# Down projection with seven products instead of eight, its operand sums made in gate and up, a new pool layout and row sums of squares

## The chip, the cores and the metric

The kernel runs on one core of a Trainium2 chip. The metric is the time of one execution on the device in microseconds. The kernel is a whole layer stack of two blocks for 512 tokens of width 2048; the change touches only its last part: the second output projection, the gate and up projections of the second block's feed-forward network, and the down projection with the final norm.

## The reference, cut to what matters

All arrays are float32. After the second block's mixer the reference computes, with `x` the residual stream of 512 x 2048 and `h` the mixer's output:

```python
x = x + h @ w_out_2                              # second output projection
y = rmsnorm(x, norm2_g_2)
u = silu(y @ ffn_w_gate_2) * (y @ ffn_w_up_2)    # 2048 -> 5632, gate and up
x = x + u @ ffn_w_down_2                         # 5632 -> 2048, down
out = rmsnorm(x, final_norm_g_2)
```

`rmsnorm` divides a row by the root of its mean square (plus 1e-6) and multiplies by a weight for each column.

## The kernel before, in words

Every float32 product is made of three matmuls in the fp32r type. Each operand is split into a high part (a cast by ScalarE, `split` at L136) and a low part (what is left, a subtraction by VectorE, `tt` at L122), and high x high, high x low and low x high are summed in PSUM. Weights come as blocks of 256 x 512 (a tile of 128 x 1024, 512 KB) on SP's DMA queue and are split into `wh` and `wl`, here called a weight half. Instructions are put in order by a scheduler that follows priorities (`high_priority`), and each engine then works through its own list in order. Two tiles of different pools may lie at the same bytes when their lifetimes don't overlap; the later one waits for the earlier.

`finish` holds the part that matters here.

- **Second output projection.** Four blocks of 512 features (b = 0, 2, 1, 3). For each, TensorE makes four tiles of 128 features x 512 tokens; VectorE adds the residual (`xr`), scales to `z`, and TensorE turns the tile to token rows, which ScalarE copies to `xs` and a DMA writes to `x3d`. The sum of squares of each token is collected in feature layout: ScalarE squares each tile, VectorE adds it to `s3` (`squares`), and at the end eight small matmuls with ones and `token_rsq` give `r3`. After each pair of blocks `fast_operands` builds the operands of the seven products for gate and up.
- **Gate and up.** Eleven chunks of 512 hidden features. Each product of a 2 x 2 block matrix is made by seven block products instead of eight (`fast_group`), with the sums of raw weights made by VectorE in place (`chained`) and the results combined from PSUM. `X` holds the operands, `fr` the raw weights, ten buffers; the weight halves rotate over three buffers (`wps`: two of `wp2`, one of `fw`). The activations come out in token rows, are turned by TensorE and written as 4 x 11 feature tiles to `ud` in DRAM.
- **Down.** `hidden(c)` reads a chunk of `ud` and splits it. `down(c, hs)` goes over four column blocks of 512; for each, `block` loads two weight halves and makes 4 row tiles x 4 token tiles x 3 matmuls, and VectorE adds the four PSUM tiles to `facc`, which starts as the residual read back from `x3d`. The weight halves rotate over the two buffers of `wp2`, the raw weights over three. The last chunk has its weights split ahead, and goes token tile by token tile with the final norm behind it.

Of the kernel before, what the change touches and what calls it, by code (L numbers as in the profile page):

```python
# [8 lines left out]
F32 = mybir.dt.float32  # L9
F32R = mybir.dt.float32r  # L10
# [7 lines left out]
D = 2048  # L18
# [75 lines left out]
class Kernel:  # L94
# [1508 lines left out]
    def fast_operands(self, pool, za, zb, tiles):  # L1603
        ta, tb = slice(0, 256), slice(256, 512)
        x5 = self.t(pool, [128, 4, 256], F32, "fx5")
        x6 = self.t(pool, [128, 4, 256], F32, "fx6")
        x7 = self.t(pool, [128, 4, 256], F32, "fx7")
# [4 lines left out]
        for i, x in ((1, za[:, :, ta]), (7, x7), (5, x5), (6, x6), (4, None), (3, zb[:, :, tb]), (2, zb[:, :, ta])):  # L1612
            if i == 4:
                x = x7
                self.tt(x, zb[:, :, ta], x6, ALU.add)
# [7 lines left out]
    def halves(self, raw, pools):  # L1623
# [4 lines left out]
        return h, l  # L1628

    def fast_group(self, srcs, X, rp, cp, wps, parts):
# [22 lines left out]
        def part(i, u, opens):  # L1655
            with tc.high_priority(self.ahead):
                h, l = self.halves(weight[i](u), wps)
            at = [(2 * u + kk, kk, t) for kk in range(2) for t in range(2)]

            for j, kk, t in at:  # L1660
                xh, xl = (x[:, j % 4, t * 128:t * 128 + 128] for x in X[j // 4][i])
                self.mm(ps[i][:, t, :], xh, h[:, kk, :], opens and j == 0, False, not opens)
                self.mm(ps[i][:, t, :], xl, h[:, kk, :], False, False, not opens)
            for j, kk, t in at:
                xh = X[j // 4][i][0][:, j % 4, t * 128:t * 128 + 128]
                self.mm(ps[i][:, t, :], xh, l[:, kk, :], False, j == 7, not opens)
# [43 lines left out]
    def finish(self):  # L1710
        tc, nc, a = self.tc, self.nc, self.a
        NC = 11
        ud = self.t(self.dr, [4 * NC, 128, NX], F32, "ud")
        x3d = self.t(self.dr, [4, 128, D], F32, "x3d")
        wg, wu, wd = a["ffn_w_gate_2"][0], a["ffn_w_up_2"][0], a["ffn_w_down_2"][0]
        with self.pool("ff0", 1) as f0:
# [3 lines left out]
            with self.pool("opx", 2) as opx:  # L1720
                X = []
                made = [0]

# [4 lines left out]
                with self.pool("w21", 1) as p1, self.pool("w22", 2) as p2, self.pool("w23", 3) as p3:  # L1728
                    s3 = self.t(p1, [128, NX], F32, "s3")
                    R1 = self.token_row(p1, self.r1, "R1")  # L1730
                    za = None
                    for n, b in enumerate((0, 2, 1, 3)):
# [6 lines left out]
                        for j in range(4):  # L1739
# [6 lines left out]
                            s = self.t(p2, [128, NX], F32, "sq")  # L1746
                            self.squares(s3, x3, n == 0 and j == 0, s)
# [135 lines left out]
```

## Time and profile before

| | us |
|---|---|
| median of 3 runs | 3528.63 (3527.05 to 3533.05) |
| the profiled execution | 3531.79 |
| its span, first to last instruction | 3530.0 |
| second output projection, gate and up | TensorE changes over at about 2137 to 2155 of the span |
| gate and up, down | TensorE changes over at about 3025 to 3045 of the span |

The span of the profiled execution was recorded instruction by instruction. TensorE's granted clock was 0.985 of full speed in the mean. Busy times of TensorE overlap from one matmul to the next, so what counts there is the distance from start to start.

### The profile page before, as it was taken

The numbers are of one execution on the slowest core, as the hardware profiler recorded it, in microseconds if no ns is written. First come the engines' busy times: TensorE is split into PE (matmuls) and PEld (weight loads), VectorE is DVE, ScalarE is ACT, GpSimd is POOL, SyncE is SP. The second block draws the span as 40 slices with busy tenths as digits, with TensorE's granted clock in tenths as the row PEclk, the third lists the DMA queues.
The fourth block names the chain that finished last, engine by engine and source line by source line (L and its number), as shares of the span: only waits on it lengthen the run. The fifth ranks groups of instructions, "written<-read, shape, count | busy, mean of one in ns | idle before, by whom it ended". The sixth has DMA issues, their size and how long they took to land.

```text
span 3530.0 us, 48454 instructions
## 1 busy us (share of the span) xinstructions
PE 3438.7 (97%) x18738; PEld 2740.7 (78%) x18738; DVE 2213.8 (63%) x3495; ACT 1367.9 (39%) x2223; POOL 55.1 (2%) x50
## 2 busy tenths in 40 slices
PE   6999999999999999999999998999999999999998
PEld 3488888777778787788777786888888888788887
DVE  4367875466555455764566557778887788555545
ACT  3234444465433323433233334444444444322122
POOL 0000000000000000000000000000000000000000
PEclk8999999999999999999999999999999999999999
DMA  8833433222343443434434543444334335533333
GB/s 283 276 90 89 113 115 109 70 80 63 88 149 124 138 131 97 116 108 132 132 105 144 163 137 108 131 128 123 114 108 125 120 114 160 185 119 119 102 96 108
DMA packets 352602, 442.21 MB, mean 125 GB/s; under 512 B 45871, under 2 KB 200179, under 8 KB 351731
## 3 DMA queue, kind: packets, MB, share of 16 engines
q1 hardware_dynamic: 349456, 437.82, 40.8%
q8 instruction: 147, 2.41, 0.3%
q10 hardware_dynamic: 2915, 1.29, 0.1%
q14 instruction: 84, 0.69, 0.1%
HBM read 383.45 MB, written 55.57 MB: 124 GB/s over the span
## 4 chain that ended last, share of the span: by engine, by line
PE 90%; DMA 5%; DVE 3%; issue 1%; ACT 1%; SPq 0%; POOL 0%; DVEq 0%; POOLq 0%; ACTq 0%
PE acc L112 41%; PE psm L112 23%; PE pp L112 23%; DMA wm<-in_w_mod_dram 2%; PE psm L116 2%; DVE wl L122 1%; PE pt L116 1%; DMA xr<-in_x_dram 0%; DMA raw<-in_ffn_w_down_dram 0%; DVE ga L132 0%; DMA ym<-ysd 0%; DMA fr<-in_ffn_w_gate_dram 0%; DVE op L122 0%; DMA xr<-in_ctx_dram 0%; DMA fr<-in_ffn_w_up_dram 0%
## 5 line engine op out<-in xcount | busy, mean ns | idle before, releaser
L112 PE MATMUL acc<-op,wh 128*128 128x512 f32 (+2 forms) x4160 | 1245.0, 389 | 12.2 <-ACT op L136 4.1
L112 PEld LDWEIGHTS acc<-op,wh 128*128 128x128 f32 (+1 forms) x4160 | 765.1, 190 | 198.8 <-issue 32.2
L122 DVE TENSOR_TENSOR wl<-raw,wh 128x512 fp32r<-128x512 f32 (+4 forms) x464 | 420.8, 907 | 631.6 <-ACT wh L136 597.9
L112 PE MATMUL acc<-op,wl 128*128 128x512 f32 (+2 forms) x2080 | 768.3, 389 | 4.9 <-DVE wl L122 4.7
L136 ACT CAST wh<-raw 128x512 fp32r<-128x512 f32 (+4 forms) x464 | 369.1, 796 | 991.4 <-PE acc L112 597.5
L112 PE MATMUL pp<-wh,op 128*128 128x512 f32 x2112 | 529.7, 393 | 10.1 <-ACT wh L136 10.1
L136 ACT CAST wh<-fr 128x1024 fp32r<-128x1024 f32 x308 | 322.9, 1052 | 400.8 <-PE pp L112 352.8
L112 PEld LDWEIGHTS pp<-wh,op 128*128 128x128 f32 x2112 | 397.5, 188 | 98.8 <-ACT wh L136 10.2
L112 PEld LDWEIGHTS acc<-op,wl 128*128 128x128 f32 (+1 forms) x2080 | 389.7, 189 | 98.9 <-issue 18.5
L122 DVE TENSOR_TENSOR wl<-fr,wh 128x1024 fp32r<-128x1024 f32 x308 | 371.0, 1219 | 103.8 <-ACT wh L136 67.0
L112 PE MATMUL psm<-wh,op 128*128 128x512 f32 x1280 | 396.6, 391 | 7.3 <-DVE facc L122 7.3
L112 PEld LDWEIGHTS psm<-wh,op 128*128 128x128 f32 x1280 | 241.6, 189 | 58.2 <-issue 7.7
L112 PE MATMUL pp<-wl,op 128*128 128x512 f32 x1056 | 285.4, 392 | 0.1
L112 PE MATMUL psm<-wl,op 128*128 128x512 f32 x640 | 250.2, 391 | 0.3 <-DVE wl L122 0.3
L122 DVE TENSOR_TENSOR fr<-fr,fr 128x1024 f32<-128x1024 f32 x176 | 210.9, 1220 | 47.4 <-DMA fr<-in_ffn_w_gate_dram 28.8
L112 PEld LDWEIGHTS pp<-wl,op 128*128 128x128 f32 x1056 | 197.7, 188 | 43.8 <-DVE wl L122 0.8
L122 DVE TENSOR_TENSOR facc<-facc,psm 128x512 f32<-128x512 f32 x176 | 117.9, 685 | 60.1 <-PE psm L112 54.3
L112 PEld LDWEIGHTS psm<-wl,op 128*128 128x128 f32 x640 | 120.8, 189 | 25.6 <-DVE wl L122 0.7
L112 PE MATMUL acc<-wh,op 128*128 128x256 f32 x576 | 113.6, 292 | 0.0
L112 PEld LDWEIGHTS acc<-wh,op 128*128 128x128 f32 x576 | 90.9, 191 | 5.0 <-issue 3.6
L112 PE MATMUL pp<-wh,opx 128*128 128x512 f32 x352 | 93.8, 399 | 0.0
L112 PE MATMUL acc<-wl,op 128*128 128x256 f32 x288 | 84.4, 294 | 1.0 <-DVE wl L122 0.9
(474 smaller groups left out, 3521.3 us busy)
## 6 DMA issues: line engine op xcount, KB each, us to landing
raw<-in_w_in_dram SPq DMA_DIRECT2D x216, 256.0 KB, 2.8
fr<-in_ffn_w_gate_dram SPq DMA_DIRECT2D x88, 512.0 KB, 4.2
fr<-in_ffn_w_up_dram SPq DMA_DIRECT2D x88, 512.0 KB, 4.2
raw<-in_ffn_w_down_dram SPq DMA_DIRECT2D x88, 512.0 KB, 4.0
wm<-in_w_mod_dram SPq DMA_DIRECT2D x64, 512.0 KB, 5.5
raw<-in_w_out_dram SPq DMA_DIRECT2D x64, 512.0 KB, 3.8
raw<-in_w_in_dram SPq DMA_DIRECT2D x240, 128.0 KB, 2.3
wm<-in_w_mod_dram SPq DMA_DIRECT2D x64, 256.0 KB, 2.9
```

The source lines that it names most:

```text
L112: self.nc.tensor.matmul(out, lhsT=l, rhs=r, start=start, stop=stop, skip_group_check=more)
L116: self.nc.tensor.transpose(out, x, self.ident[0:n, 0:n])
L122: (e or self.nc.vector).tensor_tensor(out=out, in0=x, in1=y, op=op)
L136: self.nc.scalar.copy(h, x)
```

## The change

**Down projection.** The chunks 0 to 9 are taken in five pairs. The hidden features of a pair and the tokens form a 2 x 2 block matrix, and so do the weights of a pair and a column half of 1024; the four output blocks are made of seven block products of half size in place of eight. A product is two weight halves of 12 matmuls each (`product`, taken out of `fast_group`). The order is 1, 7, 2, 5, 4, 6, 3; products 2, 4 and 3 go onto the PSUM of 1, 7 and 5. The results are added to `facc` and to `au`, a tile that is needed by three of the four blocks and is added to (or taken from) them after the last pair. In the first pair most results are copied by ScalarE instead of added, and the residual is added to `facc` afterwards by accumulating DMAs from POOL's queue.

**Sums of weights.** The products 7, 6 and 3 need a11 plus a21, then plus a22, then plus a12. These sums are made in the tile of a11 by accumulating DMAs out of DRAM on POOL's queue (`plus`), each after the product before has read the tile. a21 + a22 for product 5 is summed by VectorE (`both`).

**Operand sums.** The sums of hidden features that the products need are made in gate and up from the turned activations (`x5`, `x6`, `b12`, `b21`), and `ud` is written and read in seven parts. `operands` loads them into `fr` buffers and splits them.

**Pools.** `fr` stays open through down, where it also takes the place of the pool of raw weights; the PSUM pools of gate and up stay as well. In the second output projection the pools are opened in another order (`z3` first, the `fx` tiles in a pool of their own, `xr`, `xs` and `sq` last), and down's weight halves rotate over three buffers.

**Sums of squares.** ScalarE squares the token rows in `xs` with a sum along the row (`accum_out`), four for each block, and one reduction and one power give `r3`. `s3`, VectorE's additions and the matmuls with ones are gone.

```diff
-    def fast_operands(self, pool, za, zb, tiles):
+    def fast_operands(self, temps, za, zb, tiles, order=(1, 7, 5, 6, 4, 3, 2)):
...
+        x5, x6, x7 = temps(), temps(), temps()
...
+    def product(self, X, i, ps, h, l, j0, opens, last):
+        at = [(j0 + kk, kk, t) for kk in range(2) for t in range(2)]
+
+        for j, kk, t in at:
+            xh, xl = (x[:, j % 4, t * 128:t * 128 + 128] for x in X[j // 4][i])
+            self.mm(ps[:, t, :], xh, h[:, kk, :], opens and j == 0, False, not opens)
+            self.mm(ps[:, t, :], xl, h[:, kk, :], False, False, not opens)
+        for j, kk, t in at:
+            xh = X[j // 4][i][0][:, j % 4, t * 128:t * 128 + 128]
+            self.mm(ps[:, t, :], xh, l[:, kk, :], False, j == last, not opens)
...
-        ud = self.t(self.dr, [4 * NC, 128, NX], F32, "ud")
+        ud = self.t(self.dr, [7, NC, 2, 128, 256], F32, "ud")
...
-                with self.pool("w21", 1) as p1, self.pool("w22", 2) as p2, self.pool("w23", 3) as p3:
-                    s3 = self.t(p1, [128, NX], F32, "s3")
+                with self.pool("w23", 3) as p3, self.pool("w24", 1) as p4, self.pool("w21", 1) as p1, self.pool("w22", 2) as p2:
+                    s4 = self.t(p1, [128, 4, 4], F32, "s4")
...
-                            s = self.t(p2, [128, NX], F32, "sq")
-                            self.squares(s3, x3, n == 0 and j == 0, s)
...
+                        for t in range(4):
+                            self.act(self.t(p2, [128, 512], F32, "sq"), xs[:, t, :], AF.Square, accum_out=s4[:, t, n:n + 1])
...
-                            X.append(self.fast_operands(p1, za, z, tiles))
-                    r = self.token_rsq(f0, s3, D, 1e-6, "r3s")
-                    nc.vector.tensor_copy(r3, r)
+                            X.append(self.fast_operands(lambda: self.t(p4, [128, 4, 256], F32, f"fx{next(fx) % 3}"), za, z, tiles))
+                    nc.vector.tensor_reduce(out=r3, in_=s4, axis=AX.X, op=ALU.add)
+                    self.rsq(r3, r3, D, 1e-6)
...
-                with self.pool("fr", 10, side="right") as rp, self.pool("fc", 1) as cp, self.pool("fu", 2) as up, self.pool("fw", 1) as fw:
+                self.raw_pool = self.pool("fr", 10, side="right")
+                rp = self.raw_pool.__enter__()
+                with self.pool("fc", 1) as cp, self.pool("fu", 2) as up, self.pool("fv", 4) as uv, self.pool("fw", 1) as fw:
...
+                            vs = [self.t(uv, [128, 2, 256], F32, "v") for _ in range(2)]
                             for k in range(2):
-                                v = self.t(up, [128, 2, 256], F32, "v")
-                                nc.scalar.copy(v, pt[k].rearrange("p (f t) -> p f t", f=2))
-                                f = c * 4 + k * 2
-                                nc.sync.dma_start(out=ud[f:f + 2, :, half * 256:half * 256 + 256].rearrange("f p t -> p f t"), in_=v)
-            self.raw_pool = self.pool("wq", 3, side="right")
-            self.wp = self.raw_pool.__enter__()
-            self.psum_pools(4, 4)
+                                nc.scalar.copy(vs[k], pt[k].rearrange("p (f t) -> p f t", f=2))
+                            if half:
+                                b12, b22 = vs
+                                continue
+                            b11, b21 = vs
+                            out = [(1, b11), (2, b21), (3, b22)]
+                            if c < NC - 1:
+                                x5, x6 = (self.t(up, [128, 512], F32, "s").rearrange("p (f t) -> p f t", f=2) for _ in range(2))
+                                self.tt(x5, b11, b12, ALU.subtract)
+                                self.tt(b12, b12, b22, ALU.subtract)
+                                self.stt(x6, b22, -1.0, x5, ALU.mult, ALU.subtract)
+                                out += [(5, x5), (7, b12), (6, x6)]
+                            else:
+                                out.append((5, b12))
+                            for i, x in out:
+                                nc.sync.dma_start(out=ud[i - 1, c].rearrange("f p t -> p f t"), in_=x)
+                            if c < NC - 1:
+                                self.tt(b21, b21, x6, ALU.add)
+                                nc.sync.dma_start(out=ud[3, c].rearrange("f p t -> p f t"), in_=b21)
...
+                wps = [self.wp2, self.wp2, p2]
...
+                au = [self.t(p2, [128, 2, 512], F32, f"au{v}") for v in range(2)]
...
+                order = (1, 7, 2, 5, 4, 6, 3)
+
+                def operands(c):
+                    X = {}
+                    with tc.high_priority(400):
+                        for i in order:
+                            x = raw().rearrange("p a (b t) -> p (a b) t", t=256)
+                            nc.sync.dma_start(out=x, in_=ud[i - 1, 2 * c:2 * c + 2].rearrange("g f p t -> p (g f) t"))
+                            o = self.four(F32R)
+                            h, l = (o[:, k:k + 2, :].rearrange("p a (b t) -> p (a b) t", t=256) for k in (0, 2))
+                            self.split(h, l, x)
+                            X[i] = (h, l)
+                    return [X]
...
+                def down(c, v, X):
+                    n1 = slice(v * 1024, v * 1024 + 512)
+                    n2 = slice(v * 1024 + 512, v * 1024 + 1024)
+                    W = {}
+                    ps = {}
+
+                    def load(name, u):
+                        k = ((c * 2 + u) * 4 + (2 if name[2] == "2" else 0)) * 128
+                        return wd[k:k + 256, n1 if name[1] == "1" else n2].rearrange("(k p) c -> p k c", p=128)
+
+                    def plain(name, u):
+                        W[name, u] = raw()
+                        nc.sync.dma_start(out=W[name, u], in_=load(name, u))
+                        return W[name, u]
+
+
+                    def plus(name, u):
+                        nc.gpsimd.dma_start(out=W["a11", u], in_=load(name, u), accum_op=ALU.add)
+                        return W["a11", u]
+
+                    def both(u):
+                        x, y = plain("a21", u), plain("a22", u)
+                        self.tt(x, x, y, ALU.add)
+                        return x
+
+                    weight = {
+                        1: lambda u: plain("a11", u), 7: lambda u: plus("a21", u), 2: lambda u: plain("a12", u),
+                        5: both, 4: lambda u: W["a22", u], 6: lambda u: plus("a22", u), 3: lambda u: plus("a12", u),
+                    }
+                    A11, A12, A21, A22, U = acc[:, 0:2, n1], acc[:, 2:4, n1], acc[:, 0:2, n2], acc[:, 2:4, n2], au[v]
+                    onto = {2: 1, 4: 7, 3: 5}
+                    to = {1: U, 7: A22, 2: A11, 5: A22, 4: A21, 6: U, 3: A12}
+                    for i in order:
+                        ps[i] = ps[onto[i]] if i in onto else bank()
+                        for u in range(2):
+                            with tc.high_priority(self.ahead):
+                                h, l = self.halves(weight[i](u), wps)
+                            self.product(X, i, ps[i], h, l, 2 * u, i not in onto, 3)
+                        if c == 0 and i not in (5, 6):
+                            nc.scalar.copy(to[i], ps[i])
+                        else:
+                            self.tt(to[i], to[i], ps[i], ALU.subtract if i == 5 else ALU.add)
+                    if c == 0:
+                        for t in range(4):
+                            o = slice(v * 1024, v * 1024 + 1024)
+                            nc.gpsimd.dma_start(out=acc[:, t, o], in_=x3d[t][:, o], accum_op=ALU.add)
+                    if c == NC // 2 - 1:
+                        self.tt(A21, A21, U, ALU.subtract)
+                        self.tt(A22, A22, U, ALU.subtract)
+                        self.tt(A12, A12, U, ALU.add)
+
+                X = operands(0)
+                for c in range(NC // 2):
+                    down(c, 0, X)
+                    down(c, 1, X)
+                    if c + 1 < NC // 2:
+                        X = operands(c + 1)
...
-                def down(c, hs):
+                    for i, f, o in ((1, 0, 0), (5, 0, 256), (2, 2, 0), (3, 2, 256)):
+                        nc.sync.dma_start(out=u[:, f:f + 2, o:o + 256], in_=ud[i - 1, c].rearrange("f p t -> p f t"))
+                    uh, ul = self.four(F32R), self.four(F32R)
+                    self.split(uh, ul, u)
+                    W = []
                     for b in range(4):
-                        ps = [self.psm() for _ in range(4)]
-                        self.block(wd[c * 512:c * 512 + 512], [(b * 512, 512)], 4,
-                                   [(ps[t], "t", (t, 0), hs, True, True) for t in range(4)])
-                        for t in range(4):
-                            v = acc[:, t, b * 512:b * 512 + 512]
-                            self.tt(v, v, ps[t], ALU.add)
-
-                hs = [hidden(0), hidden(1)]
-                for c in range(NC - 1):
-                    down(c, hs[c])
-                    if c + 2 < NC:
-                        hs.append(hidden(c + 2))
...
+                    fg = []
+                    for i in range(2):
+                        fg.append(raw())
+                        nc.sync.dma_start(out=fg[i].rearrange("p a b -> p (a b)"),
+                                          in_=a["final_norm_g_2"][i * 1024:i * 1024 + 1024].rearrange("(o d) -> o d", o=1).to_broadcast([128, 1024]))
```

## Rows read from the trace of the kernel before

**Rows 1.** The page: busy times with instruction counts, and the chain by line
```profile
PE 3438.7 (97%) x18738; PEld 2740.7 (78%) x18738; DVE 2213.8 (63%) x3495; ACT 1367.9 (39%) x2223; POOL 55.1 (2%) x50
...
PE acc L112 41%; PE psm L112 23%; PE pp L112 23%; DMA wm<-in_w_mod_dram 2%; PE psm L116 2%; DVE wl L122 1%; PE pt L116 1%; DMA xr<-in_x_dram 0%; DMA raw<-in_ffn_w_down_dram 0%; DVE ga L132 0%; DMA ym<-ysd 0%; DMA fr<-in_ffn_w_gate_dram 0%; DVE op L122 0%; DMA xr<-in_ctx_dram 0%; DMA fr<-in_ffn_w_up_dram 0%
```

**Rows 2.** Windows: length, busy us (x count) by engine, PEclk, DMA share, GB/s
```profile
2700.00:2800.00 100.00, 100.00 (x449) 81.90 (x448) 84.10 (x80) 46.62 (x52) 0.00 (x0) 1.00 0.36 111
...
3100.00:3200.00 100.00, 100.00 (x443) 82.84 (x442) 50.99 (x58) 22.59 (x20) 0.00 (x0) 1.00 0.40 118
```

**Rows 3.** Timeline, ScalarE, down: start, duration, instruction, idle before
```profile
3396.78 1.05 ACT L136 CAST wh<-raw 128x1024 fp32r<-128x1024 f32 x1 [4.38 <-DVE facc L122]
3402.22 1.05 ACT L136 CAST wh<-raw 128x1024 fp32r<-128x1024 f32 x1 [4.38 <-PE psm L112]
```

**Rows 4.** Timeline, TensorE, gate and up: first and last of four halves
```profile
2949.11 2.01 PE L112 MATMUL pp<-wh,op 128*128 128x512 f32 x8
...
2957.35 2.01 PE L112 MATMUL pp<-wh,op 128*128 128x512 f32 x8
```

**Rows 5.** Groups by form, down: xcount, busy us, mean ns, idle before
```profile
L122 DVE TENSOR_TENSOR facc<-facc,psm 128x512 f32<-128x512 f32 x173 | 115.9, 685 | 52.2 <-PE psm L112 52.2
L122 DVE TENSOR_TENSOR wl<-raw,wh 128x1024 fp32r<-128x1024 f32 x76 | 93.0, 1224 | 164.6 <-ACT wh L136 164.5
L136 ACT CAST wh<-raw 128x1024 fp32r<-128x1024 f32 x76 | 80.1, 1054 | 305.2 <-PE psm L112 197.0 <-DVE facc L122 108.3
```

**Rows 6.** Groups by form, gate and up
```profile
L122 DVE TENSOR_TENSOR fr<-fr,fr 128x1024 f32<-128x1024 f32 x165 | 197.9, 1220 | 47.3 <-DMA fr<-in_ffn_w_gate_dram 28.8 <-DMA fr<-in_ffn_w_up_dram 17.6
...
L122 DVE TENSOR_TENSOR c<-pp,un 128x1024 f32<-128x1024 f32 x11 | 13.4, 1216 | 0.0
```

**Rows 7.** Timeline where gate and up begins
```profile
2142.77 0.68 DVE L122 TENSOR_TENSOR s<-s,sq 128x512 f32<-128x512 f32 x1
...
2149.12 1.21 DVE L122 TENSOR_TENSOR fx<-z,fx 128x1024 f32<-128x1024 f32 x1
...
2150.41 0.88 SPq L1640 DMA_DIRECT2D fr<-in_ffn_w_gate_dram  x2
...
2154.38 1.04 ACT L136 CAST wh<-fr 128x1024 fp32r<-128x1024 f32 x1 [2.97 <-DMA fr<-in_ffn_w_gate_dram]
...
2155.48 3.78 PE L112 MATMUL pp<-wh,op 128*128 128x512 f32 x8 [10.11 <-ACT wh L136]
```

**Rows 8.** One window of the same stretch
```profile
2150.00:2160.00 10.00, 4.52 (x11) 3.58 (x12) 6.31 (x9) 3.86 (x4) 1.20 (x1) 0.52 0.85 306
```

**Rows 9.** Timeline where down begins
```profile
3025.51 0.47 PE L112 MATMUL pp<-wl,opx 128*128 128x512 f32 x1
...
3034.38 0.88 SPq L1787 DMA_DIRECT2D ud<-v  x2
...
3045.15 0.77 PE L112 MATMUL psm<-wh,op 128*128 128x512 f32 x1 [7.34 <-DVE facc L122]
```

**Rows 10.** DMA issues: queue, count, KB each, median us to landing
```profile
raw<-in_ffn_w_down_dram SPq DMA_DIRECT2D x88, 512.0 KB, 4.0
...
ud<-v SPq DMA_DIRECT2D x44, 256.0 KB, 2.2
op<-ud SPq DMA_DIRECT2D x11, 1024.0 KB, 6.9
...
facc<-x3d SPq DMA_DIRECT2D x4, 1024.0 KB, 9.0
```

**Rows 11.** Windows of strong DMA traffic
```profile
30.00:40.00 10.00, 3.66 (x17) 2.66 (x17) 4.70 (x11) 4.92 (x12) 1.33 (x1) 0.66 0.98 306
2154.00:2158.00 4.00, 2.52 (x6) 2.04 (x7) 2.34 (x2) 2.09 (x2) 0.00 (x0) 0.50 1.05 398
```

**Rows 12.** Groups by form, POOL, whole span
```profile
L122 POOL TENSOR_TENSOR r<-r,mhalf 128x4 f32<-128x4 f32 x4 | 4.7, 1184 | 1126.2 <-DVE r L129 1126.1
...
L122 POOL TENSOR_TENSOR r3s<-r3s,mhalf 128x4 f32<-128x4 f32 x1 | 1.9, 1867 | 188.1 <-DVE r3s L129 188.1
```

More of the change, by code (lines that the diff above doesn't have):

```diff
@@ L1657, in part @@
                 h, l = self.halves(weight[i](u), wps)
[L1658 to L1666, printed above, removed]
+            self.product(X, i, ps[i], h, l, 2 * u, opens, 7)
         def bank():
@@ L1722, in finish @@
                 made = [0]
+                fx = iter(range(100))
                 def tiles():
@@ L1795, in finish @@
-                fg = self.t(p2, [128, D], F32, "fg")
-                nc.sync.dma_start(out=fg, in_=a["final_norm_g_2"].rearrange("(o d) -> o d", o=1).to_broadcast([128, D]))
-                def hidden(c):
-                    u = self.four(F32)
-                    nc.sync.dma_start(out=u, in_=ud[c * 4:c * 4 + 4].rearrange("f p t -> p f t"))
-                    h4, l4 = self.four(F32R), self.four(F32R)
-                    self.split(h4, l4, u)
-                    return [(h4[:, j, :], l4[:, j, :]) for j in range(4)]
@@ L1815, in finish @@
-                for c in range(NC - 1):
-                    down(c, hs[c])
-                    if c + 2 < NC:
-                        hs.append(hidden(c + 2))
-                c = NC - 1
-                W = []
-                for b in range(4):
-                    h4, l4 = self.four(F32R), self.four(F32R)
-                    for k in range(0, 4, 2):
-                        raw = self.t(self.wp, [128, 2, 512], F32, "raw")
-                        nc.sync.dma_start(out=raw, in_=wd[c * 512 + k * 128:c * 512 + k * 128 + 256, b * 512:b * 512 + 512].rearrange("(k p) c -> p k c", p=128))
-                        self.split(h4[:, k:k + 2, :], l4[:, k:k + 2, :], raw)
-                    W.append((h4, l4))
+                au = [self.t(p2, [128, 2, 512], F32, f"au{v}") for v in range(2)]
@@ new lines, in raw, with bank @@
+                def raw():
+                    return self.t(rp, [128, 2, 512], F32, "fr")
+                def bank():
+                    return self.t(self.pp, [128, 2, 512], F32, "pp")
+                order = (1, 7, 2, 5, 4, 6, 3)
[10 more added lines that the diff above has]
+                    return [X]
@@ new lines, in down @@
+                def down(c, v, X):
[24 more added lines that the diff above has]
+                    to = {1: U, 7: A22, 2: A11, 5: A22, 4: A21, 6: U, 3: A12}
+                    for i in order:
+                        ps[i] = ps[onto[i]] if i in onto else bank()
[15 more added lines that the diff above has]
+                        self.tt(A12, A12, U, ALU.add)
@@ new lines, in finish @@
+                X = operands(0)
[4 more added lines that the diff above has]
+                        X = operands(c + 1)
+                c = NC - 1
+                with tc.high_priority(400):
+                    u = self.four(F32)
+                    for i, f, o in ((1, 0, 0), (5, 0, 256), (2, 2, 0), (3, 2, 256)):
[3 more added lines that the diff above has]
+                    W = []
+                    for b in range(4):
+                        h4, l4 = self.four(F32R), self.four(F32R)
+                        for k in range(0, 4, 2):
+                            r = raw()
+                            nc.sync.dma_start(out=r, in_=wd[c * 512 + k * 128:c * 512 + k * 128 + 256, b * 512:b * 512 + 512].rearrange("(k p) c -> p k c", p=128))
+                            self.split(h4[:, k:k + 2, :], l4[:, k:k + 2, :], r)
+                        W.append((h4, l4))
+                    fg = []
[3 more added lines that the diff above has]
+                                          in_=a["final_norm_g_2"][i * 1024:i * 1024 + 1024].rearrange("(o d) -> o d", o=1).to_broadcast([128, 1024]))
```

25 lines of the change are left out of this document (10 added, 15 removed).

## The prediction

> **What bounds the kernel now.** I read the page's chain first: nearly all of it is TensorE, and TensorE is busy 97% of the span [rows 1]. A busy TensorE may still be waiting on something inside a stage, so I cut the end of the span into windows of 100 us. In gate and up, and in the down projection, TensorE is busy 100 us of 100 at the full granted clock, while VectorE is busy 84 us in the one and 51 us in the other [rows 2]. So both stages go at the rate of matmuls, and what a removed matmul is worth is its spacing, not its 0.39 us of recorded duration. Two dips remain to be explained: the change from the second output projection to gate and up, and the change from gate and up to down. Their timelines are [rows 7] and [rows 9].
>
> **Fewer matmuls.** Before, down has 11 chunks x 4 column blocks x 4 row tiles x 4 token tiles x 3 terms = 2112 matmuls of 512 columns. The weight casts of one block stand 5.44 us apart in steady state, and there are 24 matmuls between them [rows 3]: 226.7 ns each, 478.8 us in all. After, five pairs of chunks x 2 column halves x 7 products x 2 weight halves x 12 matmuls = 1680, and the last chunk keeps its 192. The new matmuls have the shape and order of those in gate and up, where three weight halves (36 matmuls) start 8.24 us apart [rows 4], 228.9 ns each. So 1680 x 0.2289 + 192 x 0.2267 = 384.6 + 43.5 = 428.1 us. **Gain 51 us**, or 54.4 us if the new matmuls go at the old spacing.
>
> **What has to stay hidden behind them.** A step (one pair of chunks, one column half) is 168 matmuls, 38.4 us. In it VectorE has 14 low halves at 1.22 us [rows 5], 2 sums of raw weights at 1.22, 7 additions out of PSUM at 1.22 [rows 6], and half of the 7 operand splits of a pair, 3.5 x 1.22: 17.1 + 2.4 + 8.5 + 4.3 = 32.3 us, 84%. ScalarE has 17.5 casts at 1.05 us [rows 5], 18.4 us. Gate and up ran with VectorE at the same 84% without holding TensorE up [rows 2], so I cost this at nothing; without that cover each instruction too many is 1.2 us a step, 12 us in ten steps. Gate and up gains four more VectorE instructions of 128x512 a chunk (x5, x6, the difference in b12, the sum in b21), 4 x 0.69 [rows 5] = 2.7 us in about 80 us: VectorE goes from 84% to 87%, still under TensorE, nothing. Its seven stores of 256 KB a chunk instead of four go on SP's queue, at 2.2 us to landing [rows 10], and nobody waits for them before down.
>
> **The sums made by transfers.** Six times a step the kernel adds a weight block onto a11 by an accumulating transfer issued on POOL, and no transfer of that kind stands in the trace. Three raw sums matter: product 1 to 7 and product 6 to 3 follow each other at once, while 7 to 6 has four products between. With three weight buffers the cast of a half can start when the half three before it is through, so 2 halves (5.5 us) ahead of its own use. The cast (1.05) and the low half (1.22) then read a11; at 2.3 us the addition may start. The cast of the half two further on must be done 4 halves, 11.0 us, after the start. What is left for issue and landing is 11.0 - 2.3 - 1.05 = 7.6 us less some 0.5 for the handovers (an estimate: 0.4 us for an issue, as two stores of u take 0.88 [rows 9], and 0.06 from a cast to its matmul [rows 7]), 7.1 us; it is 5.9 us when one more 1.22 us instruction of VectorE stands before the low half. Middle: 6.5 us. For the landing itself the nearest row below is the plain load of the same 512 KB, 4.0 us, which leaves no wait; above, the four 1024 KB loads of facc queued together, 9.0 us. An addition must fetch what lies in the tile as well as the weights, so it handles the bytes of the 1024 KB load of u, 6.9 us [rows 10], and I take that: 0 to 1 us late, 0.5 us at 20 places (two a step, ten steps). **Loss 10 us**; bounds 0 and 20 x (9.0 - 6.5) = 50. Queued behind a late sum on ScalarE are the next casts, behind these the low halves, and TensorE waits for both.
>
> The Trainium skill speaks here too, against the change: "Collectives: The Full Stack", section "The bandwidth ceiling: the fold count and why AG ≠ RS ≠ AR", says that a reduction in the DMA path is half as fast as a copy because each piece needs two source reads. No run here shows an accumulating transfer; by that rule 512 KB of addition cost like 1 MB of copy.
>
> **First dip: pools and sums of squares.** The first matmul of gate and up starts at 2155.48. The chain before it: fx4 written in place over fx7 until 2150.33, then the first fr load at 2150.41, 3.9 us to land, the cast [rows 7]. That load waits for z and fx because the ten fr buffers lie where z lay. In the new layout the top of the left side holds xr, xs and sq, which are through with the last block's squares and the store of xs. Before, the last square was added at 2142.77 [rows 7]; 2142.8 + 3.9 + 1.1 = 2147.8, 7.7 us earlier. But VectorE still has the operand splits to do, so I go by its time: it loses four additions of squares in the last block, 4 x 0.68, and fills the idle 10 - 6.3 = 3.7 us of this stretch [rows 8]. **Gain 6 us**; bounds 0 (a buffer still under fx) and 7.7. The four squares by ScalarE over token rows are as many as before, and r3 is first needed at the first tanh, tens of microseconds later: nothing.
>
> **Second dip.** Before, TensorE sat 7.34 us while the first addition to facc waited for facc to be loaded [rows 9]; that load is gone, its x3d now comes by addition from POOL at the end of the first steps. But a wait takes its place: the third weight buffer of down lies, by adding up the tile sizes, where the last v tiles lay. These are free when the last stores of u have landed, 3034.38 + 0.88 + 2.2 = 3037.5 [rows 9, 10], 12 us after the last gate and up matmul at 3025.51; a cast follows. TensorE has one half (2.75 us), the transposes (1 us) and perhaps one half more to do in it: 6 to 9 us idle. I take **no change**, with bounds of +7 and -3 us.
>
> **Sum.** 51 + 6 + 0 - 10 = 47 us off the profiled execution's 3531.79 is 3484.8; the median of the runs is 3.2 us under that execution, so 3482 us.
>
> **Rivals.**
> 1. Every sum lands in time. Speaks for it: 6.9 us is within 5.9 to 7.1. 51 + 6 to 8 + 0 to 7 gives 3463 to 3472.
> 2. Transfers get short another way. A step moves 11.5 x 0.524 MB plainly and 6 x 0.524 MB by addition, 12.3 MB if these count twice. The trace shows 398 GB/s for 4 us and 306 GB/s at a DMA share of 0.98 over 10 us [rows 11]: 31 or 40.3 us a step against 38.4. At the worse, 1.9 x 10 = 19 us, 3501. Or the operand loads, which share the ten fr buffers with weights of higher priority, come after the pair has begun: 4.2 + 1.05 + 1.22 = 6.5 us at four pair borders, 26 us, 3508.
> 3. The other side: additions land too late. If one takes 9.0 us as the queued 1024 KB loads do, plus 0.7 us that POOL is held up, plus 1.3 us for one plain 512 KB in front of it (0.524 MB at 398 GB/s), it is 11.0 us: 4.5 us at 20 places, 90 us, 3562. At 9.4 us the whole gain is gone. For the 0.7: POOL's 128x4 power took 1.87 us beside busy VectorE, 1.18 us in the mean elsewhere [rows 12]. Against it: SP's loads come through at 4 us in this stage.
>
> To the 0.7 us, the Trainium skill, "SBUF — State Buffer", section "Who interferes with whom", says that a VectorE instruction with two SBUF inputs holds up GpSimd's reads, and infers that the writing of descriptors is not touched. The trace agrees with the first half by that 1.87 us. By the page, rival 3 would be 14 us less.
>
> **Numbers.** Forecast (3472 to 3497) 0.45, rival 1 0.15, rival 2 0.17, the losses just eating the gain 0.07, rival 3 0.16. A measurement of this kernel can tell about 0.2%, 7 us, from no change. Faster 0.77, same 0.07, slower 0.16. The range goes from 3458 (54.4 + 7.7 + 7.3 with no late sum, 3459) to 3540, into the mild part of rival 3.
>
> **What would show it.** Matmuls of down spaced 229 ns; additions of wl at 1.22 us with VectorE about 84%; casts wh waiting for the accumulating transfer by no more than 1 us, twice a step; the first fr load before the last fx is written, and the first matmul of gate and up no longer 5 us behind it; an idle stretch of 6 to 9 us where down begins. Wrong it would be if the accumulating transfers land after 9 us, if DMA share stands near 1 throughout down, or if TensorE waits at each pair for operands.

## The result, and the profile after

The changed kernel takes 3565.46 us in the median of four runs (3556.23 to 3567.42); the kernel before takes 3530.84 us beside it. The ratio is 1.0092, 95% interval 1.0079 to 1.0104: **slower by 0.9%, where 1.4% faster was forecast**. The profiled execution took 3567.42 us; its span is 3565.6 us, 35.6 us over that of before.

The page of the changed kernel (busy times, chain by engine), against [rows 1]:

```profile
PE 3420.5 (96%) x18490; PEld 2707.2 (76%) x18490; DVE 2307.9 (65%) x3531; ACT 1452.1 (41%) x2334; POOL 133.6 (4%) x118
...
PE 78%; DMA 9%; issue 8%; DVE 3%; ACT 1%; POOL 1%; SPq 0%; ACTq 0%; POOLq 0%; DVEq 0%
```

248 matmul records fewer, and yet a longer span: TensorE no longer carries nine tenths of the chain. Windows in down, with the columns of [rows 2], then TensorE's waits from 3015 us to the end (total us, times, longest):

```profile
3200.00:3300.00 100.00, 89.45 (x370) 71.09 (x368) 66.00 (x58) 38.86 (x39) 14.51 (x12) 0.97 0.82 206
3300.00:3400.00 100.00, 88.59 (x361) 69.31 (x362) 68.14 (x60) 40.48 (x41) 14.47 (x12) 0.97 0.81 206
```
```profile
PE pp L112 <- ACT wh L136: 65.3, 32, 5.0
PE pp L112 <- DVE wl L122: 1.9, 4, 0.5
PE pp L112 <- ACT au L1875: 1.5, 2, 1.1
```

In [rows 2] TensorE was busy 100 of 100 us in down, at a DMA share of 0.40; now it is busy 88 to 89, and the DMA share is 0.82. VectorE stands at 66 to 68%, under the 84% forecast, because it waits too (and because the forecast's 1.22 us an instruction is too much, as e6 shows below).

**Where 35.6 us went.** TensorE's timeline before (two lines), then after (three):

```profile
1948.17 0.45 PE L112 MATMUL psm<-S,op 64*64 64x64 f32 x8 [0.21 <-DVE S L122]
...
2136.47 1.47 PE L116 MATMUL psm<-ident,xr 128*128 128x128 f32 x12
```
```profile
1955.01 0.45 PE L112 MATMUL psm<-S,op 64*64 64x64 f32 x8 [0.21 <-DVE S L122]
...
2143.42 2.22 PE L116 MATMUL psm<-ident,xr 128*128 128x128 f32 x16
2155.93 3.63 PE L112 MATMUL pp<-wh,op 128*128 128x512 f32 x8 [10.29 <-ACT wh L136]
```

The last transposes of the second output projection start at 2143.42 us, against 2136.47 before: 6.9 us. These are there already at 1948 us, ahead of all that was changed; they are the wander of the stages before (the transposes start between 2134.91 and 2143.42 over the first five traces of this layout). The stretch from the transposes to gate and up is 6.5 us shorter, 12.5 us for 19.0 ([rows 7] has the 2155.48 of before). Gate and up takes 870 us as before, TensorE without a wait in it. Down, with the tail behind it, takes some 35 us more.

Down ends its matmuls 530 us after it begins: 1680 x 0.2289 + 43.5 = 428 us of matmuls at the spacing forecast, 2 us of transposes, 69 us of waits as above, and a rest of 31 us. Some 20 us of the rest are the clock. It is granted at 0.95 in the mean from 3030 to 3515 us: ten stretches of these have the lower level, 0.50, 44.4 us in sum. TensorE is busy in 39.3 of the 44.4, and at half the clock that is some 20 us of work not done; where it waits anyway, the clock costs nothing. The other 11 us stay open. The window, the sum over windows laid on the ten stretches, and TensorE's timeline where two waits end:

```profile
3030.00:3515.00 485.00, 416.24 (x1691) 326.79 (x1689) 304.99 (x264) 190.95 (x193) 78.45 (x67) 0.95 0.79 195
```
```profile
sum 44.39, PE 39.31 PEld 30.83 DVE 25.51 ACT 25.98 POOL 8.76; mean PE 3.93 PEld 3.08 DVE 2.55 ACT 2.60 POOL 0.88
```
```profile
3190.79 3.78 PE L112 MATMUL pp<-wh,op 128*128 128x512 f32 x8 [3.86 <-ACT wh L136]
3194.36 1.91 PE L112 MATMUL pp<-wl,op 128*128 128x512 f32 x4
...
3284.01 2.11 PE L112 MATMUL pp<-wh,op 128*128 128x512 f32 x8 [3.45 <-ACT wh L136]
```

Eight matmuls took 2.01 us in [rows 4]; after a wait of 3.86 us they take 3.78, at the lower of the two clock levels (granted 0.50 there), and the four behind them 1.91 instead of 1.09. So that wait of 3.9 us costs 6.5. Not every wait does it: behind the one of 3.45 us eight matmuls take 2.11.

**One late sum in full.** The same stretch of ScalarE, VectorE, POOL and TensorE, product 6 to product 3:

```profile
3209.57 1.05 ACT L136 CAST wh<-fr 128x1024 fp32r<-128x1024 f32 x1 [0.42 <-PE pp L112]
...
3209.93 2.35 DVE L122 TENSOR_TENSOR wl<-fr,wh 128x1024 fp32r<-128x1024 f32 x2
...
3214.02 1.23 DVE L122 TENSOR_TENSOR fr<-fr,fr 128x1024 f32<-128x1024 f32 x1 [1.74 <-DMA fr<-in_ffn_w_down_dram]
...
3215.16 1.22 DVE L122 TENSOR_TENSOR wl<-fr,wh 128x1024 fp32r<-128x1024 f32 x1
...
3216.68 1.20 POOL L1853 DMA_DIRECT2D fr<-in_ffn_w_down_dram  x1 [19.20 <-DVE wl L122]
...
3223.10 1.04 ACT L136 CAST wh<-fr 128x1024 fp32r<-128x1024 f32 x1 [9.70 <-DMA fr<-in_ffn_w_down_dram]
...
3224.20 2.08 PE L112 MATMUL pp<-wh,op 128*128 128x512 f32 x4 [2.72 <-ACT wh L136]
```

The cast of product 6 is done at 3210.6, but its low half starts only at 3215.16. Ahead of it in VectorE's order stand two other low halves and the sum a21+a22 of the next column half, ten weight halves before its use, which waits for its load. Only then may POOL add a12 (3216.68); that lands 6.3 us later, product 3 is cast, and TensorE has waited 2.72 us. Over all places of the stage, from these timelines (medians of 20 halves each): counted from the start of its cast, which takes 1.05 us itself, the low half starts after 2.4 us ahead of product 7, which is the cast and about one more instruction, and after 5.2 us ahead of product 3.

By the cast that ended each wait, 22 of the 69 us stand ahead of product 3 and some 30 ahead of product 7 (without the 3.69 us of the stores where down begins, see below). Some 7 us, in three places, stand behind a cast of operands that waited for its load and had a weight cast behind it in ScalarE's order. The longest (ScalarE, then TensorE):

```profile
3103.28 1.04 ACT L136 CAST op<-fr 128x1024 fp32r<-128x1024 f32 x1 [5.06 <-DMA fr<-ud]
```
```profile
3105.33 3.41 PE L112 MATMUL pp<-wh,op 128*128 128x512 f32 x8 [4.04 <-ACT wh L136]
```

DMA issues from 3000 us on, with the columns of [rows 10], and the queues there (packets, MB, share of 16 engines):

```profile
fr<-in_ffn_w_down_dram SPq DMA_DIRECT2D x88, 512.0 KB, 5.8
fr<-in_ffn_w_down_dram POOLq DMA_DIRECT2D x60, 512.0 KB, 7.1
fr<-ud SPq DMA_DIRECT2D x34, 512.0 KB, 7.1
```
```profile
q0 software_dynamic: 17472, 35.66, 37.6%
q1 hardware_dynamic: 46900, 71.55, 36.9%
```

The additions (q0, with the eight of x3d) land in 7.1 us and occupy the engines as long as all plain transfers together, with half the bytes.

### The profile page after: what moved, and what is told of

Its sections match the earlier page's. It is cut to its first block, busy times and chain, and to the rows that moved or that the text cites. A ratio compares the mean times of both kernels' runs of the same rounds, so it can differ in the third digit from the quotient of the medians.

```text
span 3565.6 us, 48437 instructions
## 1 busy us (share of the span) xinstructions
PE 3420.5 (96%) x18490; PEld 2707.2 (76%) x18490; DVE 2307.9 (65%) x3531; ACT 1452.1 (41%) x2334; POOL 133.6 (4%) x118
## 3 DMA queue, kind: packets, MB, share of 16 engines
q0 software_dynamic: 17472, 35.66, 6.0%
## 4 chain that ended last, share of the span: by engine, by line
PE 78%; DMA 9%; issue 8%; DVE 3%; ACT 1%; POOL 1%; SPq 0%; ACTq 0%; POOLq 0%; DVEq 0%
PE acc L112 40%; PE pp L112 25%; PE psm L112 10%; DMA fr<-in_ffn_w_down_dram 4%; DMA wm<-in_w_mod_dram 2%; PE psm L116 2%; DVE wl L122 1%; DMA fr<-ud 1%; PE pt L116 1%; POOL fr L1853 0%; DVE op L122 0%; ACT wh L136 0%; PE acc L116 0%; DVE ga L132 0%; DMA ym<-ysd 0%
## 5 line engine op out<-in xcount | busy, mean ns | idle before, releaser
L112 PE MATMUL pp<-wh,op 128*128 128x512 f32 x3232 | 828.5, 400 | 77.1 <-ACT wh L136 75.6
L112 PEld LDWEIGHTS pp<-wh,op 128*128 128x128 f32 x3232 | 614.1, 191 | 230.1 <-ACT wh L136 90.3
L136 ACT CAST wh<-fr 128x1024 fp32r<-128x1024 f32 x448 | 466.0, 1051 | 638.7 <-PE pp L112 413.5
L122 DVE TENSOR_TENSOR wl<-fr,wh 128x1024 fp32r<-128x1024 f32 x448 | 541.0, 1221 | 193.0 <-ACT wh L136 161.2
L122 DVE TENSOR_TENSOR wl<-raw,wh 128x512 fp32r<-128x512 f32 (+4 forms) x384 | 323.1, 842 | 469.3 <-ACT wh L136 414.9
L136 ACT CAST wh<-raw 128x512 fp32r<-128x512 f32 (+4 forms) x384 | 284.8, 742 | 691.2 <-PE acc L112 603.0
L112 PE MATMUL pp<-wl,op 128*128 128x512 f32 x1616 | 441.6, 396 | 1.9 <-DVE wl L122 1.9
L112 PEld LDWEIGHTS pp<-wl,op 128*128 128x128 f32 x1616 | 306.9, 191 | 72.3 <-DVE wl L122 4.3
L1853 POOL DMA_DIRECT2D fr<-in_ffn_w_down_dram x60 | 73.3, 1235 | 1255.2 <-DMA fr<-in_ffn_w_down_dram 891.0
L112 PE MATMUL acc<-wm,cs 128*32 128x512 f32 x256 | 65.5, 670 | 10.7 <-DMA wm<-in_w_mod_dram 10.7
```

The lines of the kernel that those rows point to most:

```text
L112: self.nc.tensor.matmul(out, lhsT=l, rhs=r, start=start, stop=stop, skip_group_check=more)
L122: (e or self.nc.vector).tensor_tensor(out=out, in0=x, in1=y, op=op)
L136: self.nc.scalar.copy(h, x)
L1853: nc.gpsimd.dma_start(out=W["a11", u], in_=load(name, u), accum_op=ALU.add)
```

## The experiments

Every ratio is against the kernel before, run beside it on the same chip; 0.1% is 3.5 us. A change is given against the changed kernel if nothing else is said.

**Chain or addition: a square of runs.** In the changed kernel a sum is chained to the low half of the product before, and it is an addition. Five runs separate the two. L1853 is the line `nc.gpsimd.dma_start(out=W["a11", u], in_=load(name, u), accum_op=ALU.add)`.

e1, no sums:
```
-  nc.gpsimd.dma_start(out=W["a11", u], in_=load(name, u), accum_op=ALU.add)
-  return W["a11", u]
+  x = raw()
+  nc.gpsimd.dma_start(out=x, in_=load(name, u))
+  return x
```


> The six sums per step are left out: products 7, 6 and 3 take a21, a22 and a12 alone, each loaded plainly by POOL into a tile of its own. Matmuls, casts, low halves and loads stay as many. Theory A (TensorE waits because a sum may start only after the low half of the product before it and its landing then comes too late for the next product): the 47 us of waiting ahead of products 7 and 3, and most of the 30 us of halved clock behind them, go: about 3490 us, 1% faster than before. Theory B (the DMA engines are the bound in down, or the operand loads are late): as many bytes are loaded, so the time stays over 3545 us.

3477.27 us, ratio 0.9854 (0.9839 to 0.9868). Theory A, and 13 us below its figure. TensorE's waits fall from 69 to 11 us. A window of it, with the columns of [rows 2]:

```profile
3200.00:3300.00 100.00, 100.00 (x437) 81.84 (x436) 77.48 (x67) 44.47 (x43) 10.11 (x14) 1.00 0.69 227
```

437 matmuls in 100 us are 229 ns each, the spacing forecast.

e2, copy in place: the line without `accum_op`.

> The accumulating transfers become plain copies on the same POOL queue into the same a11 tile, in the same chain (a11 is overwritten, so products 7, 6 and 3 take a21, a22 and a12 alone). Theory A (the whole chain cast, low half, issue, landing, cast is too long, the addition is only a part of it): landing falls from 7.1 to about 5.8 us, what SP's plain loads take, 1.3 us at 20 places and some clock: 3530 us, and TensorE still waits ahead of products 7 and 3. Theory C (it is the addition in the transfer that is slow): landing falls to 4 us as before the change, and the waits with it: about 3495 us.

3510.86 us, 0.9949 (0.9934 to 0.9964): between the two theories, so both the chain and the addition cost time. The copies land in 4.9 us, not 5.8 nor 4.0.

e10 and e13, unchained additions and their control (e13 without `accum_op`); the lines taken out are those of e1:
```
+  x = raw()
+  nc.gpsimd.memset(x, 0.0)
+  nc.gpsimd.dma_start(out=x, in_=load(name, u), accum_op=ALU.add)
+  return x
```


> The six accumulating transfers stay, but each adds onto a tile of its own that POOL has set to zero, so that none waits for a low half (products 7, 6 and 3 take one block each). Theory A (the chain, not the additions): like the run without sums, 3475 to 3490 us. Theory C2 (additions fill the DMA engines and make every other load late): over 3520 us.

> The control of the unchained additions: POOL still sets each tile to zero, and the transfer is a plain copy (products 7, 6 and 3 take one block each). If the 52 us between the run without sums and the unchained additions belong to the additions: 3475 to 3485 us. If they belong to POOL's zeroing: 3520 us or more.

e10: 3529.18 us, 0.9996 (0.9985 to 1.0008). e13: 3487.06 us, 0.9882 (0.9868 to 0.9897). Theory A alone falls, and e10 has the time of theory C2; e13 is 2 us over the figure for the additions. With no chain left, the additions cost 0.0114, 40 us. The zeroing has 0.0028, 10 us, little more than its uncertainty.

e14, each copy twice, in place of the same lines:
```
+  x = raw()
+  nc.gpsimd.dma_start(out=x, in_=load(name, u))
+  nc.gpsimd.dma_start(out=spare, in_=load(name, u))
+  return x
```


> The run without sums, with each of POOL's copies made twice, the second into a spare tile that nobody reads (products 7, 6 and 3 take one block each). Theory C3 (an addition costs what it occupies of the DMA engines, here 190 us of sixteen engines where the copies take 91, so twice a copy): as slow as the unchained additions, 3515 to 3535 us. Theory C4 (the addition itself, by its own latency or by what it does to the queue, not by engine time): under 3495 us.

3500.72 us, 0.9924 (0.9908 to 0.9941), between the theories. The queue of POOL over the whole span, in e1, e10 and e14:

```profile
q0 software_dynamic: 9792, 35.66, 3.3%
```
```profile
q0 software_dynamic: 17472, 35.66, 5.8%
```
```profile
q0 software_dynamic: 18432, 67.12, 5.8%
```

Copies made twice take the engine time of the additions, and cost 0.0070, 25 us, over e1. So engine time explains at most about 25 of the additions' 40 us; the other 15 stay open. At most, because e14 also holds its own copies back: each copy into the spare tile waits until the one before it has landed, 279 us in sum, and the next copy that is needed stands behind it on POOL:

```profile
L1856 POOL DMA_DIRECT2D spare<-in_ffn_w_down_dram x60 | 43.5, 725 | 304.4 <-DMA spare<-in_ffn_w_down_dram 279.0 <-DMA fr<-in_ffn_w_down_dram 19.9 <-DMA ud<-v 5.6
```

No run separates the two. In e10 and e14 alike, the plain loads of all other weights land late: in 4.9 us in e1, 7.8 in e14, and 8.0 in e10:

```profile
fr<-in_ffn_w_down_dram SPq DMA_DIRECT2D x88, 512.0 KB, 8.0
fr<-in_ffn_w_down_dram POOLq DMA_DIRECT2D x60, 512.0 KB, 7.8
```

The square: the additions cost 1.0092 - 0.9949 = 0.0143 chained, 50 us, and 0.0114 unchained, 40 us; the chain costs 0.9949 - 0.9854 = 0.0095 with copies, 34 us. Together 0.0238, **84 us** (each difference is sure to some 7 us).

**The chain's places.** e3, another order:
```
-  order = (1, 7, 2, 5, 4, 6, 3)
+  order = (1, 7, 2, 5, 6, 4, 3)
```


> Products in the order 1, 7, 2, 5, 6, 4, 3, so that product 4 stands between 6 and 3; nothing else changes. Theory A: the 22 us of waiting ahead of product 3 and some 12 us of halved clock behind them go, the 25 us ahead of product 7 stay: about 3532 us. Theory B (DMA bound): the order does not matter, 3560 to 3570 us.

3537.14 us, 1.0029 (1.0019 to 1.0038): 22 us less, so the order matters, and theory B falls. Theory A has the direction and two thirds of the size (it named 33 us less). TensorE's waits ahead of product 3 fall from 22 to 3 us, but all its waits only from 69 to 49, because those ahead of product 7 grow.

e9, without the sum for product 5 (`self.tt(x, x, y, ALU.add)` taken out of `both`):

> The changed kernel without VectorE's sum a21+a22 (product 5 takes a21 alone); all loads and transfers stay. Theory A2 (ahead of product 3 it is VectorE's order that makes the sum late: the low half of product 6 stands behind the next step's a21+a22, which waits for its loads): more than half of the 22 us of waiting ahead of product 3 and of the clock lost behind it goes, about 3545 us. The rival (the landing of the transfer alone makes it late): 3560 to 3567 us, as changed.

3538.98 us, 1.0022 (1.0012 to 1.0032): 25 us less; theory A2, and 6 us below its figure. VectorE's waits for loads at fr<-fr,fr, 37.9 us from 3050 to 3480 us, are gone with the instruction, though the additions land in 7.1 us as ever. Ahead of product 3 the low half now starts 2.9 us after the start of its cast, not 5.2 (medians): the place that the timeline above showed is real. With the instruction 24 us of VectorE's work went too, so the 25 us are not all its place in the order.

e12, a fourth weight buffer:
```
-  wps = [self.wp2, self.wp2, p2]
+  wps = [self.wp2, self.wp2, p2, p3]      # p3: a pool of one buffer; pool fr 9 instead of 10
```


> The changed kernel with a fourth weight buffer in down (and nine fr buffers instead of ten, for the room). If the budget for a sum is set by how far casts run ahead, as the prediction worked it out, each place gets 2.75 us more: of 47 us of waiting some 10 are left, and the clock recovers: about 3505 us. The rival: casts do not run further ahead, because they stand behind the late sum itself or the fr buffers: 3550 to 3570 us.

3659.69 us, 1.0365 (1.035 to 1.0381), far over both figures. It tells little of down: with nine fr buffers gate and up waits 57.8 us in 27 places up to 3110 us, where the changed kernel waits nowhere. From the last transposes but one to the end it takes 541 us against 536, so down gained nothing, but it too had nine buffers.

e5, VectorE makes the sum for 7 in a tile of its own, in the order of e3:
```
+  W["s", u] = raw()
+  self.tt(W["s", u], W["a11", u], plain("a21", u), ALU.add)      # 7; 6 and 3 are added onto W["s", u] by POOL
```


> VectorE adds a21 to a11 for product 7 into a tile of its own (a21 is kept for product 5), and the order is 1, 7, 2, 5, 6, 4, 3; the sums for 6 and 3 stay accumulating transfers, each now with at least one product between it and the product before it. Theory A: no sum is late any more; VectorE has 34.7 of 38.4 us a step, 90%: 3480 to 3490 us, like the run without sums. The rival: VectorE in order is the trouble (low halves wait behind other work there), and two more instructions a step make it worse: over 3510 us.

3517.1 us, 0.9952 (0.9937 to 0.9967): 27 us over theory A's upper figure, and a time that the rival named. But the rival's cause falls with e6 below, where VectorE does still more and the kernel is faster. Four additions a step are left here; at 40 to 50 us for six, four are 27 to 33 (an estimate). Over e6 it is 0.0080, 28 us.

**The first dip alone.** e4 is the kernel before with the parts of the change in `fast_operands` and in the second output projection.

> The kernel before with the new pool layout and the row sums of squares of the second output projection alone; down has eight products as before. By the prediction's step 6 us less, 3525 us (0.998). The rival: the stretch from the last output matmul to gate and up shrinks, but the unchanged stages ahead of it come out some 6 us later, as in the changed kernel's trace: 3531 us, no difference.

3524.99 us, 0.9988 (0.9979 to 0.9998): 1 to 7 us faster; the forecast of 6 lies within. In its trace 12.5 us pass from the last transposes to gate and up, as in the changed kernel, against 19.0 before.

**Other makers of the sums.** Each block is loaded once; s is a new tile. e6 has all four on VectorE, e7 all on POOL, e8 the first two on VectorE; e11 is e6 with the sum for 6 as an accumulating transfer. The four sums, with the tiles' names written out:
```
+  self.tt(s, W["a11", u], W["a21", u], ALU.add)          # 7
+  self.tt(W["a21", u], W["a21", u], W["a22", u], ALU.add) # 5
+  self.tt(s, s, W["a22", u], ALU.add)                    # 6
+  self.tt(W["a12", u], W["a12", u], s, ALU.add)          # 3
```


> No accumulating transfer: VectorE makes all four sums of a half (a11+a21 into a new tile, a21+a22, the first sum + a22, a12 + that), each block loaded once. Loads fall from 14 to 8 of 512 KB a step; VectorE gets 6 more sums of 1.22 us: 39.6 us for a step of 38.4, 103%. Theory A (late sums only): VectorE is now the bound by 1.2 us a step, 12 us and some clock, about 3495 us. Theory B (DMA bound): 3475 us or less, as the bytes fall by 40%.

> The same four sums of a half on POOL. Its one elementwise instruction near in size in the trace, 128x512, takes 1.04 us, so 128x1024 about 2.1 us, 16.8 us of 38.4 a step; VectorE falls to 29.9 us, 78%. Theory A: about 3475 us, like the run without sums. The rival: POOL is held up by VectorE and a sum takes over 4 us; then POOL is busy over 80% and the sums for 7 and 3 are late: over 3500 us.

> The same four sums, a11+a21 and a21+a22 on VectorE (34.7 us a step, 90%), the other two on POOL (8.4 us a step). Theory A: about 3475 to 3485 us; over 3500 us if a VectorE at 90% in order holds up casts and low halves.

> The sums for 7, 5 and 3 on VectorE (7 into a new tile, 3 into the a12 tile), the sum for 6 by an accumulating transfer, which has three products to land in. VectorE 37.2 of 38.4 us a step. Theory A: some 2 us a step better than all four on VectorE where VectorE bounds that, 3478 to 3485 us; the rival: the transfer's landing and its issue hold up the sum for 3 that comes behind it, 3490 to 3500 us.

**e6: 3488.12 us, 0.9872 (0.9857 to 0.9887), 1.3% faster than before: the version that beats both kernels.** The time is nearer to theory A's figure than to B's, but the run can't tell them apart: late sums and additions are both gone. A window of it, columns as above:

```profile
3200.00:3300.00 100.00, 99.01 (x430) 80.30 (x429) 93.92 (x83) 44.33 (x43) 0.00 (x0) 1.00 0.45 137
```

TensorE stands at 99 of 100 with VectorE at 94 and a DMA share of 0.45; its waits from 3015 us on are 15 us. The 103% expected took 1.22 us for each instruction, its recorded duration; but instructions that follow each other start 1.13 us apart (two low halves in 2.35 us at 3209.93 above), and 32.5 of these are 36.7 us of a step of 38.4, 96%.

e7: 3516.77 us, 0.995 (0.9935 to 0.9965); e8: 3524.26 us, 0.9977 (0.9967 to 0.9987). The times are those of the rivals, the causes are not. In e7 a sum on POOL takes 2.8 to 3.1 us in the mean, not 2.1 and not over 4, and POOL is busy 53 to 62 of 100 us, not over 80. In e8 VectorE is busy 85 to 92 of 100 us, but in e6, at 94, TensorE waits only 2 us for its low halves. Here it waits 22 us for them in each of the two runs, and the traces show that low halves take longer beside POOL's sums. Timeline of e7, POOL, then VectorE:

```profile
3215.35 6.74 POOL L1870 TENSOR_TENSOR fr<-fr,fr 128x1024 f32<-128x1024 f32 x2
```
```profile
3216.41 1.21 DVE L122 TENSOR_TENSOR facc<-facc,pp 128x1024 f32<-128x1024 f32 x1
3217.54 5.64 DVE L122 TENSOR_TENSOR wl<-fr,wh 128x1024 fp32r<-128x1024 f32 x2
```

A low half, both of whose inputs lie in SBUF, takes 2.8 us here, beside POOL, instead of 1.22 (1.94 in the mean of the stage); the addition with one input in PSUM keeps its 1.21.

e11: 3503.61 us, 0.9921 (0.9906 to 0.9936): 4 us over the rival's range. It has two additions a step, and at 40 to 50 us for six that is 13 to 17 us over e6 (an estimate); 0.0049, 17 us, were measured. Whether they are the price of the additions or the hold-up of the sum for 3 that the rival named was not separated.

## Why the prediction was wrong

**Fewer matmuls (51): right.** Where TensorE doesn't wait the new matmuls are 229 ns apart (e1). Outside waits and clock, down is 11 us over the forecast 428, not explained. e1, which has everything but the sums, comes to 0.9854; 51 + 6 with nothing lost is 0.984.

**Hidden work: right.** In gate and up there are four more VectorE instructions a chunk, and TensorE waits nowhere in the stage. In down the 84% was too high, for the reason given at e6: 26.5 instructions at 1.13 us are 29.9 of 38.4 us, 78%, and the window of e1 has 77.

**The sums made by transfers (loss 10, bounds 0 and 50): the step that failed.** The runs put 84 us there, 74 more than forecast, where the whole forecast is off by some 80. The landing was forecast well, 6.9 us against 7.1. Three other things were not.
1. "At 2.3 us the addition may start": the low half was taken to follow its cast after at most one other instruction. VectorE works in order, and the scheduler had put low halves, operand splits and the next column half's sum in front. Ahead of product 7 the low half began 2.4 us after the start of its cast, about the worse case of the prediction; ahead of product 3 it began after 5.2, some 3 us later than that. e9 takes one instruction away from there and e3 gives the place more room, for 25 and 22 us. The chain as a whole, with a transfer that lands in 4.9 us, costs 34 us.
2. An addition was priced by when it lands, not by what it keeps from others. Per byte it occupies the engines 2.04 times as long as a plain transfer (37.6% for 35.66 MB, 36.9% for 71.55 MB, above), and the plain loads land late: 40 us with no chain (e10), at most 25 of them by engine time alone (e14). This is the first half of rival 2, which allowed 19 us because it compared bytes a step with the best and a poor bandwidth. That comparison over a step does not show the delay of single loads: 4.9 us to land at a DMA share of 0.69 (e1, 3200 to 3300 us), 8.0 at 0.88 (e10, the same window). The rule that the prediction cited from the Trainium skill, "Collectives: The Full Stack", section "The bandwidth ceiling: the fold count and why AG ≠ RS ≠ AR" (an add needs two source reads, so half the speed of a copy; the page speaks of ReduceScatter), agrees with the 2.04.
3. A wait was priced at its own length. Behind some of the waits the clock was at its lower level, in ten stretches; some 20 us went that way, three tenths as much again as the 69 us of waits.

None of the three signs by which it would be wrong appeared: the additions landed in 7.1 us and not after 9, the DMA share was 0.72 to 0.90 over the 100 us windows of down and not near 1, and TensorE never waited for operands itself. They looked at the landing and at means; the loss came from the order on VectorE and from single loads that were late.

**Rival 2, second half** (operand loads late at four pair borders, 26 us): some 7 us of waits, in three places.

**Rival 3** named 3562 us, near the time measured, by an 11.0 us addition that no row shows; the time came by another way, and the nearness is luck.

**First dip (gain 6): right**, 6.5 us in the traces, 1 to 7 us by e4. The first cast waits no more for the fr load behind fx.

**Second dip (no change): right in cause, in size by luck.** Timelines of ScalarE and TensorE where down begins:

```profile
3034.29 1.04 ACT L136 CAST wh<-fr 128x1024 fp32r<-128x1024 f32 x1 [11.38 <-DMA fr<-in_ffn_w_down_dram]
...
3043.95 1.04 ACT L136 CAST wh<-fr 128x1024 fp32r<-128x1024 f32 x1 [1.70 <-DMA ud<-v]
```
```profile
3035.39 3.78 PE L112 MATMUL pp<-wh,op 128*128 128x512 f32 x8 [5.05 <-ACT wh L136]
...
3045.05 2.15 PE L112 MATMUL pp<-wh,op 128*128 128x512 f32 x8 [3.69 <-ACT wh L136]
```

The cast into the third buffer waits for the stores of u, as forecast, but TensorE loses 3.69 us by it, not 6 to 9. The 5.05 us before it are another thing, a late sum: its cast waits for a transfer of weights. The two together happen to come near the 7.34 us of [rows 9].

## What to carry to other kernels

A transfer that reads what another engine must first have read is priced from the start of that read to the next use, with every instruction that the in-order engine has in front of it, not from its landing. Ask of an added transfer also what share of the DMA engines it takes and which loads come behind it. Where an engine has room, a sum in SBUF into a tile of its own beats a transfer that sums: it frees loads as well (e6 loads 8 blocks a step instead of 14).

## What the runs showed of the hardware

- An accumulating transfer of 512 KB holds POOL for 1.24 us to issue, a plain one from the same queue 0.75 (means in e10 and e1), and takes twice the engine time.
- In e7, where both read two operands from SBUF, POOL and VectorE slow each other: 128x1024 sums of 2.8 to 3.1 us in the mean on POOL, single ones from 2.4 to 5.4; low halves of 2.8 instead of 1.22 us on VectorE. The Trainium skill, "SBUF — State Buffer", section "Who interferes with whom", says that these two kinds contend and that a VectorE instruction with at most one input in SBUF does not; e7 agrees on both. The prediction had taken from it only that GpSimd is held up; here VectorE pays as much.
- Setting 60 tiles of 128x1024 to zero on POOL, 0.98 us each, cost the kernel 10 us (e13 against e1, sure to some 7), with POOL idle three quarters of the time. Why was not tried; the plain loads land in 6.2 us instead of 4.9.
